# First stage of a two-layer hybrid diffusion step: a fixed order per engine, token statistics per partition, modulation parts in buffers of their own

## The chip, the core and the metric

The kernel runs on one core of a Trainium2 chip. A core has a matrix engine (PE, shown with its weight loads apart as PEld), a vector engine (DVE), a scalar engine (ACT), a general engine (POOL, idle here) and a sequencer (SP) that issues the transfers from memory. The engines run each their own list of instructions in order and wait for each other through semaphores. The metric is the device time of one execution in microseconds (us), the median of several.

## What is computed

One inference step of a backbone with two layers, for 128 context tokens and 512 latent tokens, model width 1024. Layer 0 mixes tokens by a bidirectional state-space scan, layer 1 by differential attention; behind each stands a gated feed-forward part with a short convolution. The change lies in the first things that layer 0 does: RMS norm of the tokens, modulation by shift and scale, and the product with the mixer's input weights.

```python
def _rms(x):
    xf = x.astype(F32)
    return xf * lax.rsqrt(jnp.mean(xf * xf, axis=-1, keepdims=True) + EPS)

def modulation(cvec, w, b):
    m = jax.nn.silu(cvec) @ w + b
    return jnp.split(m[:, None, :], 6, axis=-1)

def modulate(x, g, shift, scale):
    return rmsnorm(x, g) * (1 + scale) + shift
...
hp = modulate(xp, norm_mix_g[i], p_sh1, p_sc1)
hs = modulate(xs, norm_mix_g[i], s_sh1, s_sc1)
...
proj = h @ in_w          # inside ssd_mixer
```

`xp` are the context tokens, modulated from `c_ctx`; `xs` the latent tokens, modulated from `c`. All is f32.

## The kernel before

Activations lie transposed: features on the 128 partitions, the 640 tokens (512 latent, then 128 context) along the row. The width 1024 makes eight blocks (`KT = 8`), so x is eight tiles of 128x640, and the normed, modulated input h eight more. Each h block is kept as two f32r tiles whose sum is the value, a high half `h00h` and a low half `h00l`; each weight tile likewise as `whi` and `wlo`. One f32 product is then three f32r products (high by high, low by high, high by low), each over tokens 0 to 255 and 256 to 639: six matmuls for a weight tile and a block of h, 256 and 384 columns in turn. `dense_many` writes them out.

The first stage is `first_tiles`. It loads c, constants, x, the first weight tile (`w_dt`, 64 outputs), and the modulation weights of the first shift and scale, cut into four parts of 2 MB (part q serves h blocks 2q and 2q+1), each as eight transfers of 256 KB. It computes:

- the token statistics: squares of x on ACT and DVE in turn (`sq`), summed over the features by products with a matrix of ones (`ms`, four products of 160 tokens side by side in the array, 32 columns of it each), then rsqrt by nine DVE operations on 128x160 (`rsqrt`), then a product that spreads it over all partitions (`nbc`, copied to `bc` by ACT);
- the modulation rows of a part: 32 products of 32x128 with silu(c), `s32`, as weights (`modrow`), copied to SBUF by ACT (`modrow_s`), transposed by PE (`modt`), and made to `mod` and `gs` (gain times 1 plus scale) by two small DVE operations;
- h: `t = x * gs * bc` by DVE, the high half by ACT (adds the shift), the low half by DVE;
- the products of three weight tiles with h (`in`): `w_dt` and the first two tiles of the x projection, two h blocks at a time.

Behind it `ssd` goes on with the other 38 tiles of the input projection: the first one is called `x` in the trace. `ssd_consts` (small constants of the scan), the rows of the second modulation block (`mod_rows`, `mr` loads, also `modrow`) and `ssd_dt` are threaded in between.

What sets the order: the program is written once, as a sequence over all engines. A scheduler then orders each engine's list by priority and its own estimate of readiness, within what the data and the buffers allow. Buffers are named by tags with a count; a tile that takes a used buffer waits for its last reader. Parts 0 and 2 lie in buffers that `mod_slots` borrows from tags of the scan (`hs`, `qe`), parts 1 and 3 in others (`xt`, `qm`, `qc0`), so part 2 is loaded when part 0 has been read and part 3 when part 1 has. SP issues transfers strictly in its list's order and waits in line.

Helpers record most operations, so many share a line: `mm` is L103, `act` L94, `stt` L97, `tt` L100.

## Time and profile before

| | us |
|---|---|
| median of 3 runs | 1921.22 |
| lowest and highest | 1920.97, 1921.4 |
| the profiled execution | 1921.78 |
| its span, first to last instruction | 1920.0 |
| first and last transfer issue of the four parts | 8.3, 32.0 |
| first `in` product, first `x` product | 28.90, 56.69 |

The profile is one execution. Its page gives busy time by engine, the span in slices, the chain of work that ended last (followed back from the last instruction to what released it), and groups of instructions. In a row of the timeline stand start, time from the first start to the last end, engine, line, operation, output <- inputs by their names in the program, shapes, and the count of merged instructions; in brackets the idle time of the engine ahead of it and what ended it. Buffer numbers are left out. An f32 product is two instructions (passes) in the trace, an f32r product one. A matmul's time runs from its issue to the end of its result, so several overlap, and what one costs in a run is the distance of the starts.

### The profile page before, as it was taken

The page shows a single profiled execution, that of the slowest core. Times are in us where ns is not written, and L with a number is a line of the kernel's source. Part 1 is how long each engine was busy: PE and PEld are TensorE (multiplying, and loading weights), DVE is VectorE, ACT ScalarE, POOL GpSimd, SP SyncE. Part 2 cuts the span into 40 slices and gives each one's busy share as a digit, 9 for nine tenths or more (in the row PEclk, how much of TensorE's full clock was granted, in tenths as well). Part 3 has the DMA queues.
Part 4 walks back from the last instruction along what each step waited for, and adds up shares of the span by engine and source line. Part 5 has one row for each costly group of instructions (what it writes and reads, how often), then busy time and mean ns, then how long its engine had stood idle before and what let it go on. Part 6 is the DMA issues. An engine that isn't in the chain of part 4 may idle for free.

```text
span 1920.0 us, 33586 instructions
## 1 busy us (share of the span) xinstructions
PE 1887.8 (98%) x13741; PEld 1781.4 (93%) x13741; DVE 1377.3 (72%) x2649; ACT 944.5 (49%) x1753; POOL 0.2 (0%) x4
## 2 busy tenths in 40 slices
PE   7999999999999999999999999999999999999997
PEld 4899898989989999999999989888899999999997
DVE  4779998989847999994455877788677553553554
ACT  3468585858525542343343566666446432441441
POOL 0000000000000000000000000000000000000000
PEclk9999999999999999999999999999999999999998
DMA  9612112123452556642222211111032222222211
GB/s 341 230 56 67 56 55 78 45 67 101 158 173 78 181 181 206 208 138 75 77 68 76 86 38 50 49 46 34 13 121 80 77 77 78 65 68 88 72 40 55
DMA packets 66730, 185.01 MB, mean 96 GB/s; under 512 B 8336, under 2 KB 14736, under 8 KB 66448
## 3 DMA queue, kind: packets, MB, share of 16 engines
q1 hardware_dynamic: 66000, 182.34, 29.3%
q8 instruction: 108, 1.77, 0.4%
q10 hardware_dynamic: 576, 0.52, 0.1%
q14 instruction: 46, 0.38, 0.1%
HBM read 177.06 MB, written 5.77 MB: 95 GB/s over the span
## 4 chain that ended last, share of the span: by engine, by line
PE 94%; DVE 2%; DMA 1%; ACT 1%; issue 0%; SPq 0%; DVEq 0%; ACTq 0%
PE up L103 30%; PE po L103 25%; PE z L103 6%; PE x L103 5%; PE st L103 5%; PE bc L103 3%; PE yp L103 3%; PE v L103 3%; PE q L103 2%; PE sl L103 2%; PE k L103 2%; PE ov L103 1%; PE modrow L103 1%; PE r L103 1%; PE wt L1052 1%; PE in L103 1%
## 5 line engine op out<-in xcount | busy, mean ns | idle before, releaser
L94 ACT ACTIVATE whi<-raw 128x1024 fp32r<-128x1024 f32 (+4 forms) x230 | 236.0, 1027 | 414.4 <-PE po L103 243.7
L100 DVE TENSOR_TENSOR wlo<-raw,whi 128x1024 fp32r<-128x1024 f32 (+4 forms) x230 | 270.3, 1177 | 183.8 <-ACT whi L94 178.1
L97 DVE SCALAR_TENSOR_TENSOR xr<-po,mod,xr 128x256 f32<-128x256 f32 (+2 forms) x231 | 89.0, 434 | 159.0 <-PE po L103 158.8
L103 PE MATMUL po<-mh,whi 128*128 128x256 f32 (+1 forms) x704 | 167.5, 310 | 0.0
L103 PE MATMUL po<-ml,whi 128*128 128x256 f32 (+1 forms) x704 | 167.2, 309 | 0.0
L103 PE MATMUL po<-mh,wlo 128*128 128x256 f32 (+1 forms) x704 | 167.0, 309 | 0.0
L103 PE MATMUL up<-h01h,wlo 128*128 128x256 f32 (+1 forms) x656 | 149.4, 308 | 0.0
L103 PE MATMUL up<-h11h,wlo 128*128 128x256 f32 (+1 forms) x656 | 149.4, 308 | 0.0
L103 PE MATMUL up<-h01h,whi 128*128 128x256 f32 (+1 forms) x656 | 149.3, 308 | 0.0
L103 PE MATMUL up<-h11h,whi 128*128 128x256 f32 (+1 forms) x656 | 149.3, 308 | 0.0
L103 PE MATMUL up<-h01l,whi 128*128 128x256 f32 (+1 forms) x656 | 149.3, 308 | 0.0
L103 PE MATMUL up<-h11l,whi 128*128 128x256 f32 (+1 forms) x656 | 149.3, 308 | 0.0
L103 PEld LDWEIGHTS po<-mh,whi 128*128 128x128 f32 x704 | 128.3, 188 | 0.6 <-ACT mh L94 0.4
L103 PEld LDWEIGHTS po<-mh,wlo 128*128 128x128 f32 x704 | 128.6, 188 | 0.0
L103 PEld LDWEIGHTS po<-ml,whi 128*128 128x128 f32 x704 | 128.4, 188 | 0.0
L103 PEld LDWEIGHTS up<-h01h,wlo 128*128 128x128 f32 x656 | 119.3, 188 | 0.0
L103 PEld LDWEIGHTS up<-h11h,wlo 128*128 128x128 f32 x656 | 119.3, 188 | 0.0
L103 PEld LDWEIGHTS up<-h11h,whi 128*128 128x128 f32 x656 | 119.3, 188 | 0.0
L103 PEld LDWEIGHTS up<-h01h,whi 128*128 128x128 f32 x656 | 119.3, 188 | 0.0
L103 PEld LDWEIGHTS up<-h01l,whi 128*128 128x128 f32 x656 | 119.3, 188 | 0.0
L103 PEld LDWEIGHTS up<-h11l,whi 128*128 128x128 f32 x656 | 119.2, 188 | 0.0
L97 DVE SCALAR_TENSOR_TENSOR ca<-uraw,fcw,ca 128x511 f32<-128x511 f32 (+1 forms) x176 | 85.2, 546 | 11.7 <-ACT ca L94 11.7
(505 smaller groups left out, 4469.2 us busy)
## 6 DMA issues: line engine op xcount, KB each, us to landing
raw<-in_w_up SPq DMA_DIRECT2D x88, 512.0 KB, 3.5
mw<-in_modT SPq DMA_DIRECT2D x48, 512.0 KB, 3.6
raw<-in_w_in SPq DMA_DIRECT2D x40, 512.0 KB, 3.5
raw<-in_w_dn SPq DMA_DIRECT2D x32, 448.0 KB, 3.3
raw<-in_w_qkv SPq DMA_DIRECT2D x24, 512.0 KB, 3.5
mr<-in_mod SPq DMA_DIRECT2D x44, 256.0 KB, 5.4
raw<-in_w_so SPq DMA_DIRECT2D x16, 512.0 KB, 4.1
raw<-in_w_dn SPq DMA_DIRECT2D x16, 512.0 KB, 3.7
```

The costliest lines, as they stand in the source:

```text
L94: return self.nc.scalar.activation(out, in_, func, **k)
L97: return self.nc.vector.scalar_tensor_tensor(out, in0, s, in1, op0, op1)
L100: return self.nc.vector.tensor_tensor(out, a, b, op)
L103: return self.nc.tensor.matmul(out, lhsT, rhs, start=start, stop=stop)
L1052: nc.tensor.transpose(pm[:, b * P:(b + 1) * P], ws[b][:, kc * P:(kc + 1) * P], self.ident)
```

## The change

The modulation weights are laid out as four arrays of 128 x 8 x 512, so that a part comes in two transfers of 1 MB, and each part gets a buffer of its own in a new pool (`first`), which is given back when the stage ends. The whole stage stands outside the scheduler (`manual_schedule`): each engine's list is the order of the text. The statistics become products with x squared as weights and one column of ones as moving operand, five per block of x, so that the sums of 128 tokens lie on the partitions, 128x5 in all; the rsqrt works on 128x5, is followed by a multiplication with 3/8 (which sat in the constant `sel` before), and is spread by five products of 128x128. x is multiplied with it first (`scaled`), so that ACT applies scale and shift in one step, and DVE scales the same tile in place and subtracts. `ssd_consts`, a second load of c with its silu, and `mod_rows(1)` now come behind the stage, in the pool `ssd`.

```diff
+    def silu_cond(self, pool):
+        c32 = pool.tile([P, KT, 32], F32, tag="c32", name="c32", bufs=1)
+        self.nc.sync.dma_start(c32, self.a["c32"])
+        self.s32 = pool.tile([P, KT, 32], F32, tag="s32", name="s32", bufs=1)
+        self.silu_small(self.s32, c32)
...
     def first_tiles(self, h, pool):
...
+        def load(q, halves=2):
+            parts[q] = pool.tile([P, KT, 512], F32, tag="mp", name=f"mp{q}", bufs=4)
+            n = KT // halves
+            for k in range(0, KT, n):
+                nc.sync.dma_start(parts[q][:, k:k + n, :], a["modp"][q, :, k:k + n, :])
...
+        def scaled(i):
+            t0[i] = self.tmp("h0")
+            self.tt(t0[i], self.x[i], bc, ALU.mult)
+
+        def apply(i):
+            t = t0.pop(i)
+            for a0, b0, c in cond:
+                self.act(h[i][0][:, a0:b0], t[:, a0:b0], AF.Identity, scale=gs[:, i, c:c + 1], bias=sh[:, i, c:c + 1])
+            for a0, b0, c in cond:
+                nc.vector.tensor_scalar(t[:, a0:b0], t[:, a0:b0], gs[:, i, c:c + 1], sh[:, i, c:c + 1], ALU.mult, ALU.add)
+            self.tt(h[i][1], t, h[i][0].bitcast(F32), ALU.subtract)
...
-        self.prefetch(0)
+        self.prefetch(1)
         self.load_consts()
...
         load(0)
         self.prefetch(2)
-        load(1)
...
+        for q in range(1, 4):
+            load(q)
+        self.prefetch(3)
+        ms = self.bank("m", "ms")
         for i in range(KT):
+            s = self.slot("f", f"sq{i}", bufs=NF)
             if i % 2:
-                self.tt(sq[i], self.x[i], self.x[i], ALU.mult)
+                self.tt(s, self.x[i], self.x[i], ALU.mult)
             else:
-                self.act(sq[i], self.x[i], AF.Square)
+                self.act(s, self.x[i], AF.Square)
+            for j in range(NCH):
+                self.mm(ms[:, j:j + 1], s[:, j * P:(j + 1) * P], self.ones[:, :1], i + j == 0, i + j == KT + NCH - 2)
+        y = self.pc.tile([P, 160], F32, tag="rs_y", name="rs_y", bufs=2)[:, :NCH]
+        self.rsqrt(y, ms[:, :NCH], NCH, D)
+        nc.vector.tensor_scalar(y, y, 3.0 / 8, None, ALU.mult)
+        bps = self.dense_ps("nbc")[:, 128:128 + T]
+        for j in range(NCH):
+            self.mm(bps[:, j * P:(j + 1) * P], y[:, j:j + 1].to_broadcast([P, P]), self.ident, True, True)
+        self.cast(0)
+        self.cast(1)
         bc = self.slot("f", "bc", bufs=NF)
         self.act(bc, bps, AF.Copy)
+        scaled(0)
+        scaled(1)
         h.extend(self.new_h("h00"))
+        rows(0, 0, KT)
+        finish(0)
+        apply(0)
+        self.cast(2)
...
+        apply(1)
+        for q in range(3):
+            k = 2 * q
+            dense(ws, k)
+            rows(q + 1, 0, KT // 2 if q == 0 else KT)
+            scaled(k + 2)
+            dense(ws[:2], k + 1)
+            if q == 0:
+                rows(1, KT // 2, KT)
+            else:
+                finish(q + 1)
+                apply(k + 2)
+            scaled(k + 3)
+            dense(ws[2:], k + 1)
+            if q == 0:
+                finish(1)
+                apply(2)
+            apply(k + 3)
...
-        dtps, tmod = self.first_tiles(h, pool)
+        self.ssd_consts(pool)
+        self.silu_cond(pool)
+        tmod = self.add(self.mod_rows(1, pool, 7))
...
+        with tc.tile_pool(name="first", bufs=1) as pool, tc.manual_schedule():
+            dtps = self.first_tiles(hs[0], pool)
         with tc.tile_pool(name="ssd", bufs=1) as pool:
-            self.ssd(hs[0], norm(0, 1, hs[1]), pool)
+            self.ssd(hs[0], dtps, norm(0, 1, hs[1]), pool)
...
-    d["modp"] = m[:, :2048].reshape(KT, P, 2, 4, 256).transpose(3, 0, 1, 2, 4).reshape(4, KT, P, 512)
+    d["modp"] = m[:, :2048].reshape(KT, P, 2, 4, 256).transpose(3, 1, 0, 2, 4).reshape(4, P, KT, 512)
```

`rows(q, k0, k1)` is the modulation product over weight blocks k0 to k1 of part q, with the copy when it is complete; `finish(q)` the transpose and the two small DVE operations; `dense(ws, k)` the `in` products of h block k.

**PE, from the last statistics to the first `in` products.** In the rows the names are output <- moving operand, weights; `mp` are the modulation weights, `s` is silu(c). Before:

```order
L103 MATMUL ms<-sq_148,cst 32x160 x4
L103 MATMUL modrow<-mp_105,s_137 32x128 x4
L103 MATMUL modrow<-mp_106,s_137 32x128 x4
L103 MATMUL modrow<-mp_107,s_137 32x128 x4
L103 MATMUL modrow<-mp_108,s_137 32x128 x4
L103 MATMUL nbc<-rs_y,cst 128x160 x2
L103 MATMUL modrow<-mp_109,s_137 32x128 x4
L103 MATMUL nbc<-rs_y,cst 128x160 x2
```

Now, at the same place:

```order
L103 MATMUL ms<-cst,sq_172 128x1 x5
L103 MATMUL ms<-cst,sq_179 128x1 x5
L103 MATMUL nbc<-cst,rs_y 128x128 x5
L103 MATMUL modrow<-mp_113,s_77 32x128 x32
L401 MATMUL modt<-cst,modrow_s 128x128
L103 MATMUL in<-h00h_219,whi_205 64x256
L103 MATMUL in<-h00h_219,whi_205 64x384
L103 MATMUL in<-h00l_220,whi_205 64x256
```

The products of part 0 stood between the statistics and the broadcast, and part 1 (not shown) ahead of the first `in`; now part 0 stands in one run behind the broadcast, and the other three parts between `in` products.

**SP, behind the loads of the modulation parts.** `scw`, `svec`, `dtb`, `ea`, `oh` and `msk` are constants of the scan, `c` the conditioning vectors, `mr` rows of the second modulation block. Before:

```order
L386 DMA mp_387<-in_modp 128x512
L123 DMA raw_445<-in_w_in 128x1024
L123 DMA raw_447<-in_w_in 128x1024
L123 DMA raw_449<-in_w_in 128x1024
L570 DMA scw<-in_scw 128x96
L573 DMA svec<-in_svec 128x32
L575 DMA dtb<-in_dtb 64x1
L577 DMA ea<-in_alog 128x64
L581 DMA ohf<-in_oh 96x32
L341 DMA mr_621<-in_mod 128x512
```

Now:

```order
L385 DMA mp_124<-in_modp 128x2048 x2
L123 DMA raw_127<-in_w_in 128x1024
L123 DMA raw_654<-in_w_in 128x1024
L123 DMA raw_656<-in_w_in 128x1024
L123 DMA raw_658<-in_w_in 128x1024
L595 DMA scw<-in_scw 128x96
L598 DMA svec<-in_svec 128x32
L600 DMA dtb<-in_dtb 64x1
L602 DMA ea<-in_alog 128x64
L369 DMA c_623<-in_c 128x256
L621 DMA msk<-in_msk 128x640
L341 DMA mr_671<-in_mod 128x512
```

The load of `scw` now takes memory of the pool `first` and waits for PE's last pass over `mp_124`, the last part; all that is listed behind it waits with it, and c is loaded a second time ahead of `mr`.

**PE, among the last `in` products.** `s_625` is the second silu(c). Now:

```order
L103 MATMUL in<-h00h_231,wlo_206 64x384
L103 MATMUL modrow<-mr_671,s_625 32x512
L103 MATMUL in<-h00h_233,whi_205 64x256
L103 MATMUL in<-h00h_233,whi_205 64x384
L103 MATMUL modrow<-mr_672,s_625 32x512
L103 MATMUL in<-h00l_234,whi_205 64x256
```

Before, all eight products of these rows stood behind the first products of the `x` tile; now one stands ahead of the last 30 `in` products and one ahead of the last 28.

More of the change, by code (lines that the diff above doesn't have):

```diff
@@ L364, in mod_rows, with rows, finish @@
         yield 1
+    def silu_cond(self, pool):
[3 more added lines that the diff above has]
+        self.silu_small(self.s32, c32)
     def first_tiles(self, h, pool):
         nc, a = self.nc, self.a
-        c32 = pool.tile([P, KT, 32], F32, tag="c32", name="c32", bufs=1)
-        nc.sync.dma_start(c32, a["c32"])
+        cond = ((0, TS, 1), (TS, T, 0))
+        t0, parts = {}, {}
+        def load(q, halves=2):
[3 more added lines that the diff above has]
+                nc.sync.dma_start(parts[q][:, k:k + n, :], a["modp"][q, :, k:k + n, :])
+        def rows(q, k0, k1):
+            if k0 == 0:
+                self.rowps = self.bank("y", "modrow")
+            for k in range(k0, k1):
+                for j in range(4):
+                    self.mm(self.rowps[32 * j:32 * j + 32, :P], self.s32[:, k, :], parts[q][:, k, j * P:(j + 1) * P],
+                            k == 0, k == KT - 1)
+            if k1 == KT:
+                self.row = self.slot("f", "modrow_s", bufs=NF)
+                self.act(self.row[:, :P], self.rowps[:, :P], AF.Copy)
+        def finish(q):
+            pt = self.bank("m", "modt")
+            nc.tensor.transpose(pt[:, :P], self.row[:, :P], self.ident)
+            i0 = 2 * q
+            mv = self.mod[0][:, 0:16, :].rearrange("p (s i) c -> p s i c", s=2)[:, :, i0:i0 + 2, :]
+            bv = self.modb[:, 0:16].rearrange("p (s i) -> p s i", s=2)[:, :, i0:i0 + 2]
+            self.tt(mv, pt[:, :P].rearrange("p (s i r) -> p s i r", s=2, i=2)[:, :, :, 0:2],
+                    bv.unsqueeze(3).to_broadcast([P, 2, 2, 2]), ALU.add)
+            self.stt(gs[:, i0:i0 + 2, :], self.mod[0][:, 8 + i0:10 + i0, :], 1.0,
+                     self.gains[:, i0:i0 + 2].unsqueeze(2).to_broadcast([P, 2, 2]), ALU.add, ALU.mult)
+        def scaled(i):
[9 more added lines that the diff above has]
+        self.silu_cond(pool)
@@ L378, in first_tiles @@
             self.x.append(xi)
-        self.prefetch(0)
+        self.prefetch(1)
         self.load_consts()
-        parts = {}
-        def load(q):
-            parts[q] = self.mod_slots(pool, q % 2, f"mp{q}")
-            for k, r in enumerate(parts[q]):
-                nc.sync.dma_start(r, a["modp"][q, k])
+        gs, sh = self.gs[0][0], self.shift(0, 0)
         load(0)
         self.prefetch(2)
-        load(1)
-        self.s32 = pool.tile([P, KT, 32], F32, tag="s32", name="s32", bufs=1)
@@ L392, in first_tiles @@
-        self.silu_small(self.s32, c32)
-        sq = [self.slot("f", f"sq{i}", bufs=NF) for i in range(KT)]
+        for q in range(1, 4):
+            load(q)
+        self.prefetch(3)
+        ms = self.bank("m", "ms")
         for i in range(KT):
+            s = self.slot("f", f"sq{i}", bufs=NF)
             if i % 2:
-                self.tt(sq[i], self.x[i], self.x[i], ALU.mult)
+                self.tt(s, self.x[i], self.x[i], ALU.mult)
             else:
-                self.act(sq[i], self.x[i], AF.Square)
@@ L400, in rows @@
-        def rows(q):
-            ps = self.bank("y", "modrow")
-            for k, r in enumerate(parts.pop(q)):
-                for j in range(4):
-                    self.mm(ps[32 * j:32 * j + 32, :P], self.s32[:, k, :], r[:, j * P:(j + 1) * P], k == 0, k == KT - 1)
-            row = self.tmp("modrow_s")
-            self.act(row[:, :P], ps[:, :P], AF.Copy)
-            return row
-        def finish(q, row):
-            pt = self.bank("m", "modt")
-            nc.tensor.transpose(pt[:, :P], row[:, :P], self.ident)
-            i0 = 2 * q
-            mv = self.mod[0][:, 0:16, :].rearrange("p (s i) c -> p s i c", s=2)[:, :, i0:i0 + 2, :]
-            bv = self.modb[:, 0:16].rearrange("p (s i) -> p s i", s=2)[:, :, i0:i0 + 2]
-            self.tt(mv, pt[:, :P].rearrange("p (s i r) -> p s i r", s=2, i=2)[:, :, :, 0:2],
-                    bv.unsqueeze(3).to_broadcast([P, 2, 2, 2]), ALU.add)
-            self.stt(self.gs[0][0][:, i0:i0 + 2, :], self.mod[0][:, 8 + i0:10 + i0, :], 1.0,
-                     self.gains[:, i0:i0 + 2].unsqueeze(2).to_broadcast([P, 2, 2]), ALU.add, ALU.mult)
@@ L421, in apply @@
-        def apply(q):
-            gs, sh = self.gs[0][0], self.shift(0, 0)
-            for i in range(2 * q, 2 * q + 2):
-                t = self.tmp("h0")
-                cond = ((0, TS, 1), (TS, T, 0))
-                for a0, b0, c in cond:
-                    self.stt(t[:, a0:b0], self.x[i][:, a0:b0], gs[:, i, c:c + 1], bc[:, a0:b0], ALU.mult, ALU.mult)
-                    self.act(h[i][0][:, a0:b0], t[:, a0:b0], AF.Identity, bias=sh[:, i, c:c + 1])
-                for a0, b0, c in cond:
-                    self.stt(h[i][1][:, a0:b0], t[:, a0:b0], sh[:, i, c:c + 1], h[i][0][:, a0:b0].bitcast(F32),
-                             ALU.add, ALU.subtract)
@@ L433, in first_tiles @@
-        st = self.rms_bcast(lambda: self.wide("nbc"), sq, 0, T, D)
-        next(st)
-        row = rows(0)
-        try:
-            next(st)
-        except StopIteration as e:
-            bps = e.value
+                self.act(s, self.x[i], AF.Square)
[3 more added lines that the diff above has]
+        self.rsqrt(y, ms[:, :NCH], NCH, D)
@@ L440, in first_tiles @@
+        nc.vector.tensor_scalar(y, y, 3.0 / 8, None, ALU.mult)
[4 more added lines that the diff above has]
+        self.cast(1)
         bc = self.slot("f", "bc", bufs=NF)
         self.act(bc, bps, AF.Copy)
+        scaled(0)
+        scaled(1)
         h.extend(self.new_h("h00"))
-        ws = []
-        for i in range(3):
-            self.cast(i)
-            ws.append((self.dense_ps("in"), self.wcast[i], P if i else 64))
@@ L447, in first_tiles @@
-        self.wi = 3
-        for q in range(4):
-            finish(q, row)
-            if q < 2:
-                load(q + 2)
-            if q < 3:
-                row = rows(q + 1)
-            apply(q)
-            if q == 1:
-                self.prefetch(5)
-                self.ssd_consts(pool)
-            if q < 3:
-                self.dense_many(ws, range(2 * q, 2 * q + 2), h, "AB", n=KT, i0=2 * q)
-        tmod = self.add(self.mod_rows(1, pool, 7))
+        rows(0, 0, KT)
+        finish(0)
@@ new lines, in first_tiles @@
+        apply(0)
+        self.cast(2)
+        ws = [(self.dense_ps("in"), self.wcast[i], P if i else 64) for i in range(3)]
+        self.wi = 3
+        dense = lambda w, k: self.dense_many(w, range(k, k + 1), h, "AB", n=KT, i0=k)
+        apply(1)
[16 more added lines that the diff above has]
+            apply(k + 3)
@@ L464, in first_tiles @@
         self.ready = [w[0] for w in ws[1:]]
-        return ws[0][0], tmod
+        return ws[0][0]
     def make_gs(self, l, s):
@@ L834, in ssd_norm, with ssd @@
             self.stt(y[t], y[t], self.svec[:, 16 + 4 * g + t:17 + 4 * g + t], bc[:, :T], ALU.mult, ALU.mult)
-    def ssd(self, h, nextnorm, pool):
+    def ssd(self, h, dtps, nextnorm, pool):
         xf = [[None] * 4 for _ in range(4)]
@@ L858, in z_tiles @@
                 zs[g].append(z)
-        dtps, tmod = self.first_tiles(h, pool)
+        self.ssd_consts(pool)
+        self.silu_cond(pool)
+        tmod = self.add(self.mod_rows(1, pool, 7))
         tdt = self.add(self.ssd_dt(dtps))
```

## The prediction, made before the change was run

> **What bounds the kernel now.** I read the page from the top. The engine totals and the chain of work that ended last come first:

> ```profile
> span 1920.0 us, 33586 instructions
> ...
> PE 1887.8 (98%) x13741; PEld 1781.4 (93%) x13741; DVE 1377.3 (72%) x2649; ACT 944.5 (49%) x1753; POOL 0.2 (0%) x4
> ...
> PE 94%; DVE 2%; DMA 1%; ACT 1%; issue 0%; SPq 0%; DVEq 0%; ACTq 0%
> ```

> The matrix engine (PE) is the path almost everywhere, so a microsecond by which the first stage ends earlier or later reaches the end nearly whole. The change touches that stage alone; behind it the listed order differs only in where a few small products sit. So the question is when PE begins the first tile behind the stage, the `x` tile. The busy time by stretch (columns: us, then busy time of PE, weight loads, DVE, ACT, POOL; granted clock, DMA share, GB/s) cuts the stage at the places that matter:

> ```profile
> 6.05:13.30 7.25, 6.05 (x64) 1.60 (x64) 3.49 (x5) 2.84 (x4) 0.00 (x0) 1.00 1.03 386
> ...
> 16.88:20.27 3.39, 3.39 (x20) 2.35 (x24) 0.00 (x0) 0.00 (x0) 0.00 (x0) 1.00 1.02 394
> 20.27:28.90 8.63, 6.08 (x106) 2.85 (x107) 5.11 (x9) 4.62 (x8) 0.00 (x0) 0.91 1.05 387
> 28.90:35.15 6.25, 6.25 (x41) 5.80 (x37) 3.29 (x9) 0.45 (x2) 0.00 (x0) 0.85 1.05 387
> 35.15:38.38 3.23, 2.77 (x78) 2.18 (x77) 0.66 (x1) 1.58 (x4) 0.00 (x0) 1.00 1.04 409
> ...
> 43.80:46.13 2.33, 1.62 (x38) 1.16 (x37) 0.01 (x1) 0.94 (x3) 0.00 (x0) 1.00 0.88 287
> 46.13:56.69 10.56, 10.55 (x72) 10.14 (x73) 8.29 (x18) 7.05 (x13) 0.00 (x0) 1.00 0.94 339
> ```

> Statistics run to 13.30, the broadcast of rstd to 20.27, the `in` products from 28.90 to 56.69, then `x`. The transfers are saturated (share about 1) until 38. The last row prices an `in` product: 36 pairs (72 matmuls) in 10.56 us, 0.293 us a pair. The stage has 72 pairs, 21.1 us, before and after. Between 28.90 and 56.69 lie 27.8 us; besides the pairs they hold 112 passes of modulation rows (48 and 64; two passes make one f32 product). These rows price the passes:

> ```profile
> L103 PE MATMUL modrow<-mp,s x176: 272/273/423, 13.3 to 44.8; 128*32 128x128 f32 x176
> ...
> 18.25 0.66 PE L103 MATMUL modrow<-mp,s 128*32 128x128 f32 x8
> ...
> 22.59 0.43 PE L103 MATMUL modrow<-mp1x,s 128*32 128x128 f32 x8 [0.16 <-DMA mp1x<-in_modp]
> 23.27 0.43 PE L103 MATMUL modrow<-mp1x,s 128*32 128x128 f32 x8 [0.25 <-DMA mp1x<-in_modp]
> ...
> 35.15 1.52 PE L103 MATMUL modrow<-mp,s 128*32 128x128 f32 x48
> ```

> Less 0.27 us, what one pass shows from start to end at least (first row), 48 passes take 1.25 us, 0.027 each; 64 take 1.75 us. The second row is the same work while PE is slow: less 0.42 us, the most one pass shows, 0.24 us remain for four passes, some 0.055 each. So 112 passes are 3.0 us, and the rest, 27.8 - 21.1 - 3.0 = 3.7 us, is what waits and slow clock now cost there. The two DMA waits 0.68 us apart say that 256 KB land every 0.68 us.

> **The change part by part.**

> *Statistics.* Now four 32-column products per x tile; after it five products with x squared as the 128-column weights and one moving column, two passes each, 80 loads in all. The loads stand in for the streaming. No row has one moving column, so the price comes from the nearest 128-column f32 loads:

> ```profile
> 6.05 0.76 PE L103 MATMUL ms<-sq,cst 128*32 128x160 f32 x8 [6.05 <-ACT sq L94]
> ...
> 12.52 0.76 PE L103 MATMUL ms<-sq,cst 128*32 128x160 f32 x8 [0.15 <-DVE sq L100]
> ...
> 16.88 0.50 PEld L103 LDWEIGHTS nbc<-rs_y,cst 128*128 128x128 f32 x2 [1.34 <-DVE rs_y L97]
> ...
> L103 PEld LDWEIGHTS nbc<-rs_y,cst x8: 288/335/338, 16.9 to 19.5; 128*128 128x128 f32 x8
> ...
> 16.88 1.44 PE L103 MATMUL nbc<-rs_y,cst 128*128 128x160 f32 x4 [0.88 <-DVE rs_y L97]
> ...
> 121.74 0.30 PEld L103 LDWEIGHTS cb<-bc,bc 128*128 128x128 f32 x2
> ...
> L103 PEld LDWEIGHTS cb<-bc,bc x40: 186/190/192, 121.7 to 483.3; 128*128 128x128 f32 x40
> ```

> Early in the run two loads end 0.50 us after the first began and the second lasts 0.337, so it began 0.163 us behind the first; later (121.74) the distance is 0.30 - 0.19 = 0.11 us. The early figure is the nearest, and I take it: 80 x 0.163 = 13.0 us. The first square is ready at the same 6.05, and a tile now needs 1.63 us where squares come some 0.9 apart, so the loads set the pace: end 19.1, with run-out 19.3, against 13.28 now (12.52 + 0.76). Bounds: nothing hidden at 0.027 a pass, the modulation passes' price (then the x tiles set the end, 13.3), and 0.265, the distance of the early broadcast products (1.44 less the last one's 0.474 leaves 0.97 us for a 0.17 lead and three distances), end 27.3.

> *rstd.* Nine operations on 160 columns become ten on 5. Chain rows now:

> ```profile
> 12.44 0.63 ACT L94 ACTIVATE whi<-raw 128x512 fp32r<-128x512 f32 x1 [0.88 <-DMA raw<-in_w_dt]
> ...
> 13.71 0.32 DVE L170 TENSOR_SCALAR rs_v<-ms 128x160 f32<-128x160 f32 x1
> ...
> 16.50 0.33 DVE L97 SCALAR_TENSOR_TENSOR rs_y<-rs_a,rs_y 128x160 f32<-128x160 f32 x1
> ...
> 20.30 0.70 ACT L94 ACTIVATE bc<-nbc 128x640 f32<-128x640 f32 x1 [7.23 <-PE nbc L103]
> 21.27 0.28 ACT L94 ACTIVATE modrow_s<-modrow 128x128 f32<-128x128 f32 x1 [0.27 <-PE modrow L103]
> ...
> 21.60 0.33 PE L412 MATMUL modt<-cst,modrow_s 128*128 128x128 f32 x1 [0.41 <-ACT modrow_s L94]
> 21.97 0.17 DVE L100 TENSOR_TENSOR mod<-modt,modb 128x8 f32<-128x8 f32 x1 [5.14 <-PE modt L412]
> 22.17 0.16 DVE L97 SCALAR_TENSOR_TENSOR gs<-mod,gains 128x4 f32<-128x4 f32 x1
> ```

> Now 3.1 us (13.71 to 16.83). Small ones start 0.20 apart (21.97, 22.17): ten are 2.0 us, 1.1 saved; rstd at 21.3. Its broadcast is ten passes of 128 columns instead of eight of 160 and in one run, since no modulation product stands between: 128/160 of 0.265 is 0.21 us each, with lead and run-out 2.4 us: 23.7. The bc copy (0.70) and the two x-times-rstd products (about 0.8 each) run beside the next step; cast 0 and 1 on ACT and DVE stand in this gap too and are done by 23.7 (0.69 and 1.2 us behind rstd).

> *Modulation part 0.* Its 64 passes now stand behind the broadcast, none between. At 0.055 and 0.027, half at each: 2.6 us, end 26.3. Its data are no limit: with one more 512 KB transfer ahead and 2 MB of its own, at 256 KB per 0.68 us behind the w_dt load (there at 12.44), they land by 19.4. The other three parts no longer wait for buffers and follow by 37, and the raw tiles behind them by 43, all ahead of their use: the eight larger transfers cost nothing. From the last pass to gs is 1.1 us today (21.25 to 22.33): gs at 27.4, against 22.33.

> *Handing over h.* Durations for the new apply:

> ```profile
> L94 ACT ACTIVATE h00h<-h,mod 128x512 fp32r<-128x512 f32 x8 | 5.7, 715 | 1.6 <-DVE h L97 1.6
> ...
> L94 ACT ACTIVATE h00h<-h,mod 128x128 fp32r<-128x128 f32 x8 | 3.2, 396 | 1.7 <-DVE h L97 1.7
> ...
> L100 DVE TENSOR_TENSOR ml<-cv,mh 128x640 fp32r<-128x640 f32 x44 | 36.3, 824 | 24.2 <-ACT mh L94 24.2
> ...
> L489 DVE TENSOR_SCALAR cbc<-cbc x2: 687/688/689, 626.8 to 627.4; 128x1024 f32<-128x1024 f32 x2
> ...
> L321 DVE TENSOR_SCALAR s<-s x1: 293/293/293, 3.6 to 3.6; 128x256 f32<-128x256 f32 x1
> ```

> High half: 0.71 behind gs (the product with rstd is already done). Low half: DVE may scale in place only when ACT has read, so 0.71 + about 0.43 (512 columns between the two TENSOR_SCALAR rows; with two column operands no row shows it, 0.75 if it goes like a three-operand one) + 0.2 + 0.82 = 2.2 us behind gs. The first `in` product starts at 28.1, 0.8 earlier than today. This is the gain the order buys; it is paid for behind it. Modulation parts 1 to 3 now all lie between `in` products, 3 x 1.75 = 5.3 us (today 3.0). And PE waits in its fixed order at each hand-over: block 0 for the low half, 2.2 - 0.7 - 0.3 = 1.2; block 2, whose transpose stands directly ahead, 0.73 (transpose to gs, 21.60 to 22.33) + 2.2 - 0.3 = 2.6; blocks 4 and 6 with six matmuls of cover (0.88), 1.75 each.

> *The end of the stage.* The constants, a second copy of c and the rows of the next modulation block now load into memory that the four parts held, so SP can issue them only behind part 3's last pass, in line. Two of these products stand ahead of the last `in` products:

> ```profile
> c<-in_c SPq DMA_DIRECT2D x1, 128.0 KB, 2.0
> ...
> 34.72 0.33 SPq L570 DMA_DIRECT2D scw<-in_scw  x1
> ...
> 36.07 0.54 SPq L575 DMA_DIRECT2D dtb<-in_dtb  x1
> 36.74 0.49 SPq L577 DMA_DIRECT2D ea<-in_alog  x1
> ...
> 38.75 5.79 SPq L341 DMA_DIRECT2D mr<-in_mod  x8
> ```

> Four issues of some 0.45, then c (landing 2.0 later), its tanh and two DVE operations (0.42, 0.43, 0.29): s32 about 6 us behind part 3. PE has 5 us of work and waits in that time. I take 0.9, and 0.3 for the last low half that queues behind s32 on DVE. The two products themselves (0.44) are gone from a later place.

> Sum behind 28.1: 21.1 + 5.3 + 1.2 + 2.6 + 3.5 + 1.2 = 34.9, so `x` at 63.0, against 56.69: **+6.3 us**. Against the profiled execution's own 1921.78 (span 1920.0) that is 1928.1; the median of the runs shown is 0.56 lower, so 1927.5.

> [...] Before its statistics end, PE is busy 6.05 of 7.25 us and the last `ms` group still takes the 0.76 of the first; only after the full stretch 16.88 to 20.27 do passes get faster. (The clock column reads 1.00 ahead of its first change; the durations say otherwise.) [...]

> **The rivals.** *A: the clock rises during the statistics.* From 10.3 on loads cost 0.11 and end at about 16.5, the broadcast 1.2 us, part 0 its 1.75: gs near 22.8, `x` 4.6 earlier than in my sum, +1.7. For it: 80 loads back to back; against it: `ms` never got faster. *B, the other side: loads with one moving column hide behind each other* at 0.027. Statistics end at 13.3 as now, part 0 is set by its data (19.4), gs at 21.8: +0.7, not slower by what can be measured. It decides at about 0.13 us a pass (10.4 us in all, 2.6 less than my sum, +3.7). If the small waits also shrink, slightly below zero. *C: the early distance is that of the broadcast products*, 0.265: +14.5. *D: the change does nothing for the time*, its moves all off the path: the chain is PE, and all moves are on PE, so I give it no share of its own beyond B's.

> **How the numbers follow.** A measurement of this kernel can tell about 0.2%, 3.8 us. My forecast (+4 to +10) gets 0.57, A (+1 to +4) 0.17, B (-4 to +3) 0.17, C (+11 to +15) 0.09. Slower by over 0.2%: nearly all of the forecast, a little of A, all of C: 0.66. Same: most of A and B: 0.28. Faster: the rest of B, 0.06. The range takes in most of B below, the slow TENSOR_SCALAR (four times 0.4) and another slow clock window in a hand-over (like 28.90 to 35.15 at 0.85) above, and stops short of C's end: 1919.5 to 1933.5.

> **What would show it.** Right: the `ms` loads about 0.16 us apart and ending near 19; part 0's rows behind 23; the first `in` near 28; gaps of 1 to 3 us ahead of the `in` products of blocks 2, 4, 6; `x` starting near 63. Wrong: loads 0.11 or less apart; the first `in` before 25; few waits between `in` products; or PE waiting anew behind 63 for rows of the second modulation block, which this sum holds to be covered.

## Result and profile after

The changed kernel takes 1941.67 us in the median of four runs (1937.93 to 1943.55), the kernel before on the same chip 1921.1. The ratio is 1.0105, 95% interval 1.0087 to 1.0123: slower by about 20 us. The forecast was 1927.5 with a range up to 1933.5, so the sign was right and the size three times too small. The profiled execution took 1939.84 us. From its page, in the order in which those lines were shown of before (span; busy time by engine; the chain that ended last):

```profile
span 1938.1 us, 33589 instructions
PE 1900.6 (98%) x13759; PEld 1798.0 (93%) x13759; DVE 1380.1 (71%) x2652; ACT 946.0 (49%) x1754; POOL 0.2 (0%) x4
PE 94%; DVE 3%; ACT 1%; DMA 1%; issue 0%; SPq 0%; DVEq 0%; ACTq 0%
```

The timeline of PE in the changed kernel through the first stage:

```profile
6.59 17.22 PE L103 MATMUL ms<-cst,sq 128*128 128x1 f32 x80 [6.59 <-ACT sq L94]
25.88 2.50 PE L103 MATMUL nbc<-cst,rs_y 128*128 128x128 f32 x10 [2.07 <-DVE rs_y L450]
28.31 3.64 PE L103 MATMUL modrow<-mp,s 128*32 128x128 f32 x64
...
33.98 0.78 PE L103 MATMUL in<-h00h,whi 128*64 128x256 f32 x2 [1.30 <-ACT h00h L94]
35.68 0.79 PE L103 MATMUL in<-h00l,whi 128*64 128x256 f32 x2 [0.93 <-DVE h00l L100]
36.27 0.73 PE L103 MATMUL in<-h00h,wlo 128*64 128x256 f32 x2
...
44.45 0.27 PE L401 MATMUL modt<-cst,modrow_s 128*128 128x128 f32 x1
46.02 0.78 PE L103 MATMUL in<-h00h,whi 128*64 128x256 f32 x2 [1.30 <-ACT h00h L94]
47.71 0.50 PE L103 MATMUL in<-h00l,whi 128*64 128x256 f32 x2 [0.92 <-DVE h00l L100]
...
66.61 0.50 PE L103 MATMUL in<-h00l,whi 128*64 128x256 f32 x2 [0.92 <-DVE h00l L100]
66.95 0.45 PE L103 MATMUL in<-h00h,wlo 128*64 128x256 f32 x2
68.34 1.02 PE L103 MATMUL modrow<-mr,s 128*32 128x512 f32 x2 [0.94 <-DMA mr<-in_mod]
69.29 0.51 PE L103 MATMUL in<-h00h,whi 128*64 128x256 f32 x2
69.73 1.04 PE L103 MATMUL modrow<-mr,s 128*32 128x512 f32 x2
70.70 0.50 PE L103 MATMUL in<-h00l,whi 128*64 128x256 f32 x2
...
74.86 0.46 PE L103 MATMUL x<-h00h,whi 128*128 128x256 f32 x2
```

The statistics end at 23.81 instead of 13.28. The first `in` product starts at 33.98 (before 28.90), `x` at 74.86 (before 56.69): 18.17 us later. Behind `x` lie 1863.2 us of the span, before 1863.3. So the loss in this execution lies ahead of `x` (to within one stretch of 3.4 us at half clock: behind `x`, up to the last 12 us, which have a granted clock of 0.5 in both, the profile of before has three of them, the changed kernel's two): 5.1 us at the first `in`, 13.1 between it and `x` (40.9 us against 27.8). The busy time by stretch (columns as before) has PE idle for 7.0 us of the 40.9, against 1.2 of 27.8 before, and a stretch at half clock (columns as in the prediction: us, busy time of PE, weight loads, DVE, ACT, POOL; granted clock, DMA share, GB/s):

```profile
31.90:35.30 3.40, 1.10 (x7) 0.40 (x3) 1.63 (x5) 2.47 (x5) 0.00 (x0) 1.00 1.00 411
35.30:38.70 3.40, 3.02 (x12) 2.93 (x13) 3.37 (x6) 1.05 (x2) 0.00 (x0) 0.51 0.95 364
45.60:49.00 3.40, 2.01 (x11) 1.52 (x12) 2.93 (x6) 1.84 (x4) 0.00 (x0) 1.00 0.00 0
49.00:52.40 3.40, 3.40 (x75) 2.99 (x74) 0.97 (x2) 0.12 (x1) 0.00 (x0) 1.00 0.00 0
33.98:74.86 40.88, 33.88 (x344) 26.95 (x345) 22.23 (x43) 14.47 (x26) 0.00 (x0) 0.96 0.39 133
```

Between 35.30 and 38.70 the granted clock is half, and the pairs of `in` stand 0.53 to 0.59 us apart (35.68 to 36.27) instead of 0.29.

### The profile page after: what moved, and what is told of

It reads as the page before. It is cut to its first block, busy times and chain, and to the rows that moved or that the text cites. A ratio compares the mean times of both kernels' runs of the same rounds, so it can differ in the third digit from the quotient of the medians.

```text
span 1938.1 us, 33589 instructions
## 1 busy us (share of the span) xinstructions
PE 1900.6 (98%) x13759; PEld 1798.0 (93%) x13759; DVE 1380.1 (71%) x2652; ACT 946.0 (49%) x1754; POOL 0.2 (0%) x4
## 4 chain that ended last, share of the span: by engine, by line
PE 94%; DVE 3%; ACT 1%; DMA 1%; issue 0%; SPq 0%; DVEq 0%; ACTq 0%
PE up L103 30%; PE po L103 25%; PE z L103 6%; PE x L103 5%; PE st L103 4%; PE bc L103 3%; PE v L103 3%; PE yp L103 3%; PE q L103 2%; PE sl L103 2%; PE k L103 2%; PE ms L103 1%; PE ov L103 1%; PE modrow L103 1%; PE in L103 1%; PE wt L1079 1%
## 5 line engine op out<-in xcount | busy, mean ns | idle before, releaser
L94 ACT ACTIVATE whi<-raw 128x1024 fp32r<-128x1024 f32 (+4 forms) x230 | 236.1, 1027 | 417.2 <-PE po L103 243.0
L100 DVE TENSOR_TENSOR wlo<-raw,whi 128x1024 fp32r<-128x1024 f32 (+4 forms) x230 | 270.5, 1178 | 184.2 <-ACT whi L94 178.5
L97 DVE SCALAR_TENSOR_TENSOR xr<-po,mod,xr 128x256 f32<-128x256 f32 (+2 forms) x231 | 89.1, 434 | 159.2 <-PE po L103 159.0
L103 PE MATMUL po<-mh,whi 128*128 128x256 f32 (+1 forms) x704 | 167.5, 310 | 0.0
L103 PE MATMUL po<-ml,whi 128*128 128x256 f32 (+1 forms) x704 | 167.3, 309 | 0.0
L103 PE MATMUL po<-mh,wlo 128*128 128x256 f32 (+1 forms) x704 | 167.0, 309 | 0.0
L103 PE MATMUL up<-h01h,wlo 128*128 128x256 f32 (+1 forms) x656 | 149.4, 308 | 0.0
L103 PE MATMUL up<-h11l,whi 128*128 128x256 f32 (+1 forms) x656 | 149.4, 308 | 0.0
L103 PE MATMUL up<-h01h,whi 128*128 128x256 f32 (+1 forms) x656 | 149.3, 308 | 0.0
L103 PE MATMUL up<-h11h,wlo 128*128 128x256 f32 (+1 forms) x656 | 149.3, 308 | 0.0
L103 PE MATMUL up<-h11h,whi 128*128 128x256 f32 (+1 forms) x656 | 149.3, 308 | 0.0
L103 PE MATMUL up<-h01l,whi 128*128 128x256 f32 (+1 forms) x656 | 149.3, 308 | 0.0
L103 PEld LDWEIGHTS po<-mh,whi 128*128 128x128 f32 x704 | 128.3, 188 | 0.6 <-ACT mh L94 0.4
L103 PEld LDWEIGHTS po<-mh,wlo 128*128 128x128 f32 x704 | 128.5, 188 | 0.0
L103 PEld LDWEIGHTS po<-ml,whi 128*128 128x128 f32 x704 | 128.4, 188 | 0.0
L103 PEld LDWEIGHTS up<-h11h,wlo 128*128 128x128 f32 x656 | 119.3, 188 | 0.0
L103 PEld LDWEIGHTS up<-h01h,whi 128*128 128x128 f32 x656 | 119.3, 188 | 0.0
L103 PEld LDWEIGHTS up<-h01l,whi 128*128 128x128 f32 x656 | 119.3, 188 | 0.0
L103 PEld LDWEIGHTS up<-h11l,whi 128*128 128x128 f32 x656 | 119.3, 188 | 0.0
L103 PEld LDWEIGHTS up<-h01h,wlo 128*128 128x128 f32 x656 | 119.3, 188 | 0.0
L103 PEld LDWEIGHTS up<-h11h,whi 128*128 128x128 f32 x656 | 119.3, 188 | 0.0
L97 DVE SCALAR_TENSOR_TENSOR ca<-uraw,fcw,ca 128x511 f32<-128x511 f32 (+1 forms) x176 | 85.3, 547 | 11.7 <-ACT ca L94 11.7
## 6 DMA issues: line engine op xcount, KB each, us to landing
mp<-in_modp SPq DMA_DIRECT2D x8, 1024.0 KB, 13.3
```

The lines of the kernel that those rows point to most:

```text
L94: return self.nc.scalar.activation(out, in_, func, **k)
L97: return self.nc.vector.scalar_tensor_tensor(out, in0, s, in1, op0, op1)
L100: return self.nc.vector.tensor_tensor(out, a, b, op)
L103: return self.nc.tensor.matmul(out, lhsT, rhs, start=start, stop=stop)
```

## Experiments

**One: the old statistics in the new order.**

```diff
-                self.mm(ms[:, j:j + 1], s[:, j * P:(j + 1) * P], self.ones[:, :1], i + j == 0, i + j == KT + NCH - 2)
+                self.mm(ms[32 * j:32 * j + 32, :n], self.ones, s[:, j * n:(j + 1) * n], i == 0, i == KT - 1)
...
+            self.mm(bps[:, j * n:(j + 1) * n], self.sel[:, j:j + 1].to_broadcast([P, P]), y, True, True)
```

> The changed kernel with the statistics of before put back: 32 columns of ones as weights and x squared as the moving side, rstd on 160 columns, nbc as four products of 160 columns; order, apply and part buffers stay as changed. Theory (80 slow weight loads hold the start back): ms ends near 13.5 instead of 23.8, the first `in` product near 24 instead of 33.98, `x` 9 to 11 us earlier than 74.86, the time about 1931. Rival (the loads are not what the start waits for, the fixed order and its hand-overs are): ms ends at 13.5 as well, but `x` moves by less than 4 us and the time stays above 1937.

Measured: 1934.76 us, 1.0065 of before (1.005 to 1.008). That lies between the theory's 1931 and the rival's 1937. By the timeline of PE the first `in` is 9.0 us earlier, as the theory has it, but `x` only 3.9, as the rival has it:

```profile
24.97 0.77 PE L103 MATMUL in<-h00h,whi 128*64 128x256 f32 x2 [1.30 <-ACT h00h L94]
...
70.95 0.46 PE L103 MATMUL x<-h00h,whi 128*128 128x256 f32 x2
```

In this execution both hold. With the old statistics the new order starts `in` 3.9 us earlier than the kernel before (28.90): that is the gain of the order. Then it takes 46.0 us to `x`, 5.1 more than the changed kernel with the same instructions. The busy time by stretch shows why:

```profile
24.97:70.95 45.98, 38.40 (x343) 30.05 (x344) 22.22 (x43) 14.55 (x26) 0.00 (x0) 0.85 0.59 220
26.20:29.60 3.40, 2.93 (x12) 2.84 (x12) 3.37 (x6) 1.15 (x3) 0.00 (x0) 0.50 1.00 417
39.80:43.20 3.40, 3.40 (x30) 3.01 (x32) 1.09 (x2) 0.00 (x0) 0.00 (x0) 0.50 0.05 22
50.10:53.50 3.40, 3.40 (x15) 3.33 (x13) 2.48 (x5) 1.20 (x2) 0.00 (x0) 0.50 0.02 5
63.70:67.10 3.40, 3.40 (x7) 0.97 (x7) 0.24 (x2) 0.00 (x0) 0.00 (x0) 0.50 0.97 299
```

Four stretches of 3.4 us (below: windows) ran at half clock, in the changed kernel's profile one. The three more, at some 1.4 us each (priced below), are 4.2 of the 5.1. So the 3.9 at `x` compares two executions with unequal clocks. Over all executions the statistics weigh more: by the ratios run one is 0.0040 faster than the changed kernel, about 7.7 us, give or take 4.5.

**Two: the new statistics alone, in the kernel before.** The products of the statistics and of the broadcast are those of the change; all else, and the scheduler, is as before.

> The kernel before with only the statistics changed (x squared as weights, one moving column, rstd on 5 columns, nbc as five products of 128); scheduler, apply and buffers as before. Theory (what the loads cost reaches the end whole, since the first `in` product waits for rstd): ms ends near 23.8, `x` 8 to 10 us later than 56.69, the time 1929 to 1931. Rival (before has slack of several us between rstd and the first `in`, set by arriving data and casts, which hides most of it): `x` later by 5 us at most, the time 1922 to 1926.

Measured: 1928.05 us, 1.0029 (1.0017 to 1.0041). The statistics end at 23.3, `in` begins at 37.33 (8.4 later), `x` at 64.30 (7.6 later), just under the theory's 8 and well over the rival's 5. The cost of the loads reaches `x` nearly whole. The median is 1928.05, between the theory's 1929 and the rival's 1926, and the profiled execution is 6.1 us longer than that of before; it has one half-clock window fewer behind `x`. The scheduler's order has few gaps behind it: 27.0 us from `in` to `x`, none of it at half clock.

**Three: PE kept busy around the statistics**, by products of 512 bf16 columns ahead of them and one behind each tile's ten passes.

```diff
+        for _ in range(14):
+            self.mm(wps, warm[:, :P], warm, True, True)
         ms = self.bank("m", "ms")
...
+            self.mm(wps, warm[:, :P], warm, True, True)
```

> The changed kernel with 14 dense bf16 products of 512 columns into an unused bank ahead of the statistics and one behind each tile's ten passes; their results are read by nobody. Theory (a pass costs 0.213 us because PE runs at half clock while it only loads weights, and dense products release the clock): passes fall to some 0.11 us, ms ends at 17 to 19 in spite of the added products, part 0 takes under 2.5 us instead of 3.64, `x` 6 to 8 us earlier than 74.86, the time 1934 to 1936. Rival 1 (0.213 us is what a load with one moving column costs at any clock): passes stay at 0.21, ms ends at 26 to 28, the time 1943 to 1946. Rival 2 (the clock rises but falls back during the loads): passes fast at first and then 0.21 again, ms ends at 20 to 25.

Measured: 1946.19 us, 1.013 (1.0113 to 1.0147). The timeline of PE (the second and third, and the fourth and last group of ten passes):

```profile
11.91 1.17 PE L103 MATMUL ms<-cst,sq 128*128 128x1 f32 x10
13.16 1.26 PE L103 MATMUL ms<-cst,sq 128*128 128x1 f32 x10
14.66 2.13 PE L103 MATMUL ms<-cst,sq 128*128 128x1 f32 x10
...
24.15 2.13 PE L103 MATMUL ms<-cst,sq 128*128 128x1 f32 x10
```

and the busy time by stretch:

```profile
10.70:14.10 3.40, 3.40 (x33) 3.34 (x32) 1.21 (x2) 1.49 (x3) 0.00 (x0) 1.00 1.08 416
14.10:17.50 3.40, 3.40 (x18) 3.22 (x18) 0.00 (x0) 0.94 (x1) 0.00 (x0) 0.50 1.01 420
```

Rival 2 is what happened, except that the statistics ended later than it said (26.3, since five groups ran slow). By the distance of the starts a pass costs 0.11 us at full clock and 0.21 at half. In the window from 10.7 PE is busy throughout by the profile, with loads, one-column passes and a few short dense products, and still the clock falls at 14.1. So this work does not hold the clock, and in the changed kernel 17.2 us of it never raised it.

**Four: the high half first at the hand-overs.** In blocks 0, 2, 4 and 6 PE does all six pairs that need only the high half, then the three with the low half.

```diff
-            dense(ws, k)
+            dense_hi_first(ws, k)
```

> The changed kernel with blocks 0, 2, 4 and 6 of the `in` products in another order: the products with the high half for all three tiles first (six pairs' worth of cover), then those with the low half. Theory (PE stands 1.4 us at each of these blocks for the low half alone): the gaps of 0.92 us ahead of the low half go, `x` is 4 to 5 us earlier than 74.86, the time about 1937. Rival (the wait only moves to the next block or to the rows of the second modulation block): `x` is less than 2 us earlier.

Measured: 1936.59 us, 1.0068 (1.0051 to 1.0085). The 0.92 us ahead of the low half are gone at all four blocks; at block 0 PE waits 0.56 us for the third weight tile instead. `x` starts at 72.06, 2.8 earlier, and from the first `in` it takes 38.3 us instead of 40.9, with two half-clock windows (35.1 to 42) instead of one. Less that window, the gain is some 4 us: the theory, at its lower end.

**Five: no row products of the second block inside the stage.**

```diff
+        nc.vector.tensor_scalar(zc, self.ready[0][:, PO:PO + 1], 0.0, None, ALU.mult)
+        self.act(self.s32, c32, AF.Tanh, scale=0.5, bias=zc)
```

> The changed kernel with the second silu(c) made to wait for the second `in` tile (its tanh takes a column of zeros, computed from that tile, as bias), so that no row product of the second modulation block stands among the `in` products; the scheduler puts all eight of the first group side by side into the `x` tile. Theory A (the wait of 1.10 us and the two lone products, 0.95 us each, are a plain loss): `x` 3.0 us earlier than 74.86, the time 2 to 3 us lower. Theory B (under them the last low half is still being made, ready at 69.83): PE then waits for that low half instead, `x` only about 0.9 us earlier, the time within 1.5 us of the changed kernel's.

Measured: 1943.43 us, 1.0112 (1.0097 to 1.0127). The waits come back at block 7, by the timeline of PE:

```profile
70.35 0.77 PE L103 MATMUL in<-h00h,whi 128*64 128x256 f32 x2 [0.79 <-ACT h00h L94]
72.05 0.80 PE L103 MATMUL in<-h00l,whi 128*64 128x256 f32 x2 [0.93 <-DVE h00l L100]
```

Four half-clock windows fell into its 44.2 us between `in` and `x`. At 1.4 us for each of the three more than in the changed kernel's profile (priced below) that leaves 40.0, a gain of 0.8: theory B. The lone products stood where PE would have waited anyway.

**Six: tensor_scalar into a tile of its own.**

```diff
-                nc.vector.tensor_scalar(t[:, a0:b0], t[:, a0:b0], gs[:, i, c:c + 1], sh[:, i, c:c + 1], ALU.mult, ALU.add)
+                nc.vector.tensor_scalar(u[:, a0:b0], t[:, a0:b0], gs[:, i, c:c + 1], sh[:, i, c:c + 1], ALU.mult, ALU.add)
```

> The changed kernel with VectorE's tensor_scalar written to a tile of its own instead of in place, so that it need not wait until ScalarE has read the same tile. Theory (that wait is half a microsecond of each hand-over): tensor_scalar starts 0.9 us earlier, the low half is ready 0.5 us earlier (the subtraction then waits for the high half), PE's 0.92 us ahead of the low half become about 0.4, `x` 1.5 to 2 us earlier than 74.86. Rival (the low half is held by the high half alone): under 0.3 us at each hand-over, `x` within 1 us.

Measured: 1935.1 us, 1.0069 (1.0053 to 1.0085). DVE's timeline:

```profile
31.02 0.80 DVE L422 TENSOR_SCALAR hu<-h,gs,mod 128x512 f32<-128x512 f32 x2
32.26 0.83 DVE L100 TENSOR_TENSOR h00l<-hu,h00h 128x640 fp32r<-128x640 f32 x1 [0.43 <-ACT h00h L94]
```

It now follows gs at once, and PE's wait for the low half is 0.47 at each of the four blocks instead of 0.92, as the theory says: 1.8 us. `x` is at 68.78, 6.1 earlier, and most of the rest is not the edit's doing. This execution's statistics began 0.65 earlier and its clock rose at 28.2 instead of 31.9, so the first `in` came 2.1 earlier; behind it no window fell to half (1.4) and only one lone product stood in PE's way.

**Seven: part 1's rows ahead of block 0.** The 64 passes stand behind `apply(1)`, ahead of the first `in`.

> The changed kernel with the 64 row products of modulation part 1 ahead of the first `in` product instead of between blocks 0 and 1. Theory (these products then fill the 1.3 and 0.9 us in which PE waits for block 0, and keep PE busy, so that no half-clock window falls on block 0): first `in` at about 36 instead of 33.98, low half without a wait, the following 2.0 us of rows gone, `x` 2 to 4 us earlier than 74.86. Rival (PE gains nothing, since the part's rows run at half clock, 3.6 us, and block 2 still waits): `x` within 1.5 us of 74.86.

Measured: 1937.38 us, 1.0083 (1.0066 to 1.01). The rows ran at full clock (1.95 us, not the 3.6 of the rival), `in` starts at 33.28 instead of the theory's 36, PE still waits 0.68 for the low half, block 0 is clear of half clock, and `x` is at 72.44, 2.4 earlier, within the theory's 2 to 4. Part of it is luck: the clock rose at 29.4 here, at 31.9 in the changed kernel's profile. Two windows then fell to half, on blocks 2 and 6.

**Eight: the gaps filled with products nobody reads**, on top of run one.

> The kernel of the first run of these (old statistics in the fixed order) with dense bf16 products nobody reads in the gaps ahead of blocks 0, 2, 4 and 6 (2 to 4 of them ahead of the high half, 2 or 3 ahead of the low half). The added products also make the scheduler put the row products of the second modulation block behind the stage, so the stretch to compare is from the first `in` product to the first low half of block 6: 35.66 us without filling (24.97 to 60.63, with three half-clock windows in it), 32.63 in the changed kernel (one window). Theory (an idle gap costs a window of 3.4 us at half clock behind it, 1.7 us, besides itself): with the gaps filled one window or none is left and the stretch is 31.5 to 33. Rival (the windows come from something else than PE's gaps): three windows stay, the stretch is 35.5 or, with the filling, up to 37.

Measured: 1933.85 us, 1.0061 (1.0046 to 1.0076). The stretch named there cannot be used: the memset for the filling stood late in DVE's list and block 0 waited 4.68 us for it. From the transpose ahead of block 2 to the first low half of block 6 it takes 22.16 us (38.64 to 60.80), in run one 25.27 (35.36 to 60.63) with two half-clock windows. With the filling there is none between 32.4 and `x`, and no window there had matmuls in less than 68% of its time. But 22.16 is also what the changed kernel's first profile takes there (44.45 to 66.61), with its gaps unfilled and no window fallen; so this one execution agrees with the theory and does not prove it. In time the run cannot be told from run one (1.0061 against 1.0065), with the 4.68 us in it.

**Nine and ten: the changed kernel again, unaltered, twice.**

> The changed kernel once more, unaltered. Theory (the clock is granted for windows of 3.413 us whose place against the program differs from run to run, and a window in which PE stood enough is followed by one at half clock): the statistics, the broadcast and all gaps between instructions are the same, but other windows fall to half; the stretch from part 1's transpose to the first low half of block 6 is 22.16 us without a window and 1.3 to 1.6 us more for each. Rival (the place of the windows is fixed by the program): the same single window at about 35.3 and `x` at 74.9 within 0.3.

> As the run before it: the changed kernel unaltered, a second sample of where the half-clock windows fall. Theory: the stretch from the first `in` product to `x` differs from 40.9 us by 1.3 to 1.6 us for each window more. Rival: the same rows as in the run before it.

Measured: 1945.44 and 1942.52 us, two runs each. The same instructions in the same order, and other windows at half clock. Stretches of the first of the two:

```profile
40.10:43.50 3.40, 3.40 (x61) 2.73 (x54) 0.00 (x0) 0.00 (x0) 0.00 (x0) 1.00 0.03 8
43.50:46.90 3.40, 1.86 (x9) 1.12 (x9) 1.27 (x5) 2.10 (x5) 0.00 (x0) 1.00 0.00 0
46.90:50.30 3.40, 2.66 (x10) 2.56 (x11) 2.96 (x5) 0.47 (x2) 0.00 (x0) 0.50 0.00 0
50.30:53.70 3.40, 3.40 (x39) 2.96 (x42) 0.00 (x0) 0.00 (x0) 0.00 (x0) 0.50 0.00 0
53.70:57.10 3.40, 3.40 (x57) 3.11 (x50) 0.20 (x2) 0.28 (x1) 0.00 (x0) 1.00 0.02 5
32.78:79.08 46.30, 39.38 (x344) 31.65 (x344) 22.24 (x43) 14.51 (x26) 0.00 (x0) 0.82 0.37 126
```

The gaps of block 2's hand-over (transpose at 44.37) begin in one window, 43.5 to 46.9, and run a little over its end: PE is busy for 1.86 of 3.40 us, and the next two windows are at half. In the profile shown first, the same gaps (44.45 to 47.71) were cut by a boundary at 45.6; that window kept 2.01 us, and nothing fell.

| execution | half-clock windows between `in` and `x` | us from `in` to `x` |
|---|---|---|
| the changed kernel, first profile | 1 | 40.88 |
| again, second | 3 | 43.66 |
| again, first | 5 | 46.30 |

That is 1.39 and 1.36 us for each window more: the theory. From the transpose ahead of block 2 to block 6 the three take 22.16 (none), 23.46 (one) and 26.40 (three).

**Eleven and twelve: a version put together from this**, with the old and the new statistics.

```diff
         apply(1)
+        rows(1, 0, KT)
+        for q in range(4):
             k = 2 * q
+            if q < 3:
+                scaled(k + 2)
+            dense_hi_first(ws, k)
+            if q < 3:
+                finish(q + 1)
+                apply(k + 2)
+                scaled(k + 3)
+                dense(ws, k + 1)
+                apply(k + 3)
+            if q < 2:
+                rows(q + 2, 0, KT)
```

> A version put together from what the runs show: the fixed order with the statistics of before, rows of part q+2 ahead of the block that hands over (so two parts' rows lead), high half first in blocks 0, 2, 4, 6, tensor_scalar into a tile of its own, third weight tile cast before part 0's rows, rows of the second modulation block behind the stage. Theory (the statistics and the hand-overs, with the half-clock windows that follow PE's gaps, are all that the change loses; the rest of the order is a gain of some 4 us at the start): first `in` near 26, no wait above 0.3 us behind it, no half-clock window between it and `x`, `x` at 51 to 53 against 56.69 in the kernel before, the time 3 to 5 us below the kernel before. Rival (DVE and ACT cannot deliver the halves faster, or the parts' transfers bound the rows): waits between the blocks stay, `x` at 55 to 58, no difference from the kernel before that can be measured.

> The same version with the statistics of the change (80 weight loads with one moving column each, rstd on 5 columns). Theory (with no waits left behind them the statistics reach the end whole): ms ends 10 us later than in the version with the old statistics, `x` 8.5 to 9.5 us later, the time 8 to 10 us above it, so about 5 us slower than the kernel before. Rival (the transfers of the parts or the casts are what the first `in` waits for, and the statistics partly hide behind them): `x` less than 6 us later.

Measured: 1916.82 us with the old statistics, 0.9975 of before (0.9966 to 0.9984), 1922.05 with the new, 1.0003 (0.9995 to 1.0012). The timeline of PE in the first:

```profile
25.93 1.08 PE L103 MATMUL modrow<-mp,s 128*32 128x128 f32 x32 [2.04 <-DMA mp<-in_modp]
26.93 0.51 PE L103 MATMUL in<-h00h,whi 128*64 128x256 f32 x2
...
52.74 0.53 PE L103 MATMUL x<-h00h,whi 128*128 128x256 f32 x2
```

`in` to `x` is 25.8 us without a wait and without a half-clock window. What the theory missed is the 2.04 us ahead of it, in which part 1's second half is still on its way. The window in which most of that wait falls (24.6 to 28.0) had matmuls in 60% of its time and was not followed by half clock; by the counts at the end, 5 in 14 such windows were. With the new statistics `x` starts at 60.19, 7.5 later, between theory (8.5 to 9.5) and rival (under 6): the broadcast starts 9.4 later, and the wait for part 1 is hidden. The time is 5.2 us above that with the old ones, less than the theory's 8 to 10.

## Why the prediction went wrong

| step (us) | predicted | profiled execution |
|---|---|---|
| statistics end | 19.3 | 23.81 |
| rstd; its broadcast | 2.0; 2.4 | 2.07; 2.43 |
| modulation part 0 | 2.6 | 3.64 |
| first `in` | 28.1 | 33.98 |
| rows of parts 1 to 3 | 5.3 | 5.8 |
| block 0; blocks 2, 4, 6 together | 1.2; 6.1 | 1.4; 7.0 |
| end of the stage | 1.2 | 3.0 |
| half clock between `in` and `x` | 0 | 1.4 |
| `x` | 63.0 | 74.86 |

**The sum failed in two places, by about six microseconds each.** Ahead of the first `in` it was 5.9 short, most of it the price of a load (4.0); behind it 6.0, where it put the half clock at nothing (1.4 in this profile, more in others) and the end of the stage at 1.2 instead of 3.0. Either alone would have left the median in the range or at its end (1927.5 + 6.0 = 1933.5); it took both.

**The loads set the statistics' pace: right, and mis-sized.** A pass costs 0.213 us, not the 0.163 taken from the first two early broadcast loads. That is 4.0 us, and the first square came 0.5 later. In the trace of before the four loads of that row begin at 16.88, 17.04, 17.31 and 17.58: the first distance is not the pace, the later ones are 0.267. Those passes move 160 columns, and 128/160 of 0.265 was the prediction's own 0.21 for a broadcast pass, which is what a load of 128 columns turned out to cost. Run three shows that the price goes with the clock: 0.11 at full, 0.21 at half. The change runs its loads at the second price: 80 in 17.2 us.

**rstd and broadcast: right**, within 0.1 us. **Part 0: mis-sized by 1.0**, all of it at half clock in this profile: the clock rises at 31.9, and the dense work only begins with the broadcast, at 25.88. In the two repeated executions it took 3.33 and 2.89.

**The hand-overs: right in place, each 0.2 to 0.4 short.** The tensor_scalar is longer than taken: by run six, its two pieces are done in 0.80 (0.55 and 0.34 by the changed kernel's trace, which overlap a little), where the sum had 0.43 and 0.2. In place it starts only when ACT has read, and that order costs 0.45 a block. Gaps of about 2.2, 1.3 and 1.3 us ahead of blocks 2, 4 and 6 stand where the prediction put them.

**The end: too low by 1.8.** A lone row product takes 0.95 us (68.34 to 69.29), where I had 0.44 for two; in the kernel before, sixteen passes (eight products) in a row, on four column groups, take 1.92 (59.20 to 61.12). Run five shows that only about 0.8 of it can be had back, because the last low half comes no sooner.

**The half clock: put at nothing.** The sum took each gap of PE for what it lasts and no more. But gaps that fill enough of a window go with half clock in the next (the counts are at the end). The range allowed for one more slow window; the three profiled executions had one, three and five, at 1.4 us each. The profile shown first was the mildest of the three, and its 1939.84 us lie below the other two's times. The small rest, about 1.2 us of the 40.9, is in the main pauses of some 0.1 at the seams between rows, transposes and `in` products.

**The rivals.** A (the clock rises under the loads) and B (they hide) fell: in the changed kernel `ms` never got faster than 0.21. No run shows the rise at 10.3 that A took, three windows of 3.41 us ahead of 20.5, where the clock record of the trace of before begins. C's 0.265 was as far from 0.213 on the other side as the forecast's 0.163; even its sum, +14.5, lacked the windows. That nothing is lost behind `x` held, to within the one half-clock window in which the two profiles differ there.

So of the 18.2 us, run one puts 9.0 on the statistics at the first `in`; the order gains 3.9 there and loses 13.1 behind it, by gaps and the clock. Over all executions, by the ratios, the order costs some 12.5 us (run one against the kernel before) and the statistics the other 7.7. The last two runs put the parts together the other way, with the hand-overs mended: without gaps behind the first `in` a fixed order gains 4 us at `x`, and the new statistics cost 7.5 (in the median times, 5 each).

## What to carry to other kernels

Where PE is the bound, a list in fixed order should have work that is ready ahead of every hand-over: rows of the next part, products that need only the half that comes first. A gap can be paid twice, for what it lasts and by 1.4 us for a window at half clock behind it, and several short ones within 3.4 us add up (1.54 us of the window from 43.5 to 46.9 in the first of the repeated executions, and two windows at half clock behind it). One profile shows one placement of the windows: compare the granted clock by stretches in several executions before naming a cause. Turning streaming into weight loads (80 loads of 128 columns for one column each) is dear where PE runs at half clock: 0.21 us a load here.
